# A tiled two-layer decoder in float32: the split of the Strassen weight differences is tied behind the next ordinary tile's split

## The chip, the cores and the metric

The kernel runs on one core of one Trainium2 chip. The metric is the device time of one execution in microseconds, as a median over runs. Five engines work side by side, each on its own list of instructions in the order of that list, with semaphores between them: TensorE (PE, matrix products; PEld is its loading of weights), VectorE (DVE), ScalarE (ACT), GpSimd (POOL) and SyncE (SP), which here issues the weight transfers.

## The reference

Two layers on 256 tokens of width 2048, all in float32. Layer 0 is a recurrent block (RG-LRU), layer 1 is sliding-window attention; behind each stands a gated feed-forward block. The change lies in the first matrix product of that block alone.

```python
def swiglu_ffn(x, g, w_in, w_out):
    h = rms_norm(x, g)
    gate, up = jnp.split(h @ w_in, 2, axis=-1)
    return x + (jax.nn.silu(gate) * up) @ w_out
```

## The kernel before

**Split products.** Each weight tile of 128x1024 float32 comes from memory into one of four buffers `raw0` to `raw3`. ACT casts it into `hi` (type fp32r), DVE subtracts `raw - hi` into `lo`, and each product is made of three matmuls: hi by hi, hi by lo, lo by hi. `hi` and `lo` have four buffers each, used in turn, so tile i+4 may only be cast when PE has done with tile i, and raw tile i+4 may only be loaded when ACT, DVE and POOL have read tile i.

**Strassen tiles.** In the product with `w_in` of each feed-forward block, the first four of 22 groups of output features (`NS = 4`) are computed with seven block products in place of eight. Each of these 32 *Strassen tiles* (four groups of eight) needs differences of its weight blocks: POOL makes two 128x512 tiles out of `raw` in three operations (`sums`, L279 to L281), ACT casts each (L288), DVE subtracts (L289). These land in one of two sets of buffers. A Strassen tile's own cast and split cover 768 columns only (`split`, L297 and L298); an ordinary tile's cover 1024 (L303 and L306). A Strassen tile has 21 matmuls (L472), an ordinary one 24 (L371). On PE one Strassen tile and one ordinary tile alternate (`OWN = 1`); I call two such neighbours a *pair*, and eight pairs a *group*. Within a Strassen tile in the middle of a group (L462 and L463) the first nine matmuls need `lo` and `hi` alone, the next six the first difference tile, the last six the second.

**Around a group's end.** When a Strassen group has ended, DVE combines four PSUM banks (`fast`: `s<-b,t` and `s<-b,s` at L132, then two L136). When a group of ordinary tiles has ended, DVE has a *burst* of six small operations, four `h<-b,rstd` that read PSUM and two `s<-h,h`. The Strassen tiles also need sums of the activations (`form`, L501 to L504 on POOL, a cast on ACT and a subtraction on DVE), which are made in advance, the last two while the first Strassen tiles run.

**What sets the order.** `stream` walks through all tiles: at step i it writes the load of tile i+4, then the split of tile i+3, then the split of the differences of tile i+2, then the products of tile i, with background tasks between. A scheduler then orders the instructions of each engine by its own estimate of when their inputs are there; the order written out is a priority, not the result. `issue_after(x)` ties the instructions written under it behind x, on the engine of x.

Of the kernel before, what the change touches and what calls it, by code (L numbers as in the profile page):

```python
# [12 lines left out]
F32 = mybir.dt.float32  # L13
F32R = mybir.dt.float32r
AF = mybir.ActivationFunctionType
ALU = mybir.AluOpType
# [33 lines left out]
class Trunk:  # L50
# [232 lines left out]
    def split_sums(self, i):  # L283

        if len(self.jobs[i]) > 2:
            s = self.jobs[i][2]["set"]
            for z, a, b in ((s[0], s[2], s[3]), (s[1], s[4], s[5])):
                self.nc.scalar.activation(a, z, AF.Copy)  # L288
                self.nc.vector.tensor_tensor(b, z, a.bitcast(F32), ALU.subtract)  # L289
            self.dve += 1400  # L290
            self.act += 1200

    def split(self, i):
        raw, hi, lo = self.raw[i % 4], self.hi[i % 4], self.lo[i % 4]
        if len(self.jobs[i]) > 2:
            q = slice(T, 1024)
            self.nc.scalar.activation(hi[:, q], raw[:, q], AF.Copy)  # L297
            self.nc.vector.tensor_tensor(lo[:, q], raw[:, q], hi[:, q].bitcast(F32), ALU.subtract)  # L298
            return
        n = 512 if i < 3 else 1024  # L300
        for c in range(0, 1024, n):
            q = slice(c, c + n)
            high = self.ins(self.nc.scalar.activation(hi[:, q], raw[:, q], AF.Copy))  # L303
            if i == 1:
                self.opening = high
            self.nc.vector.tensor_tensor(lo[:, q], raw[:, q], hi[:, q].bitcast(F32), ALU.subtract)  # L306

    def warm(self):

# [1059 lines left out]
```

## Time and profile before

| | us |
|---|---|
| median of three runs | 2023.03 (2022.57 to 2026.29) |
| the profiled execution | 2024.98 |
| its span, first to last instruction | 2023.2 |
| PE busy | 1983.6 (98%) |
| DVE busy | 1421.7 (70%) |
| ACT busy | 1126.1 (56%) |
| POOL busy | 384.5 (19%) |

The profile has the program's time line in 40 slices; POOL is busy in two stretches, the two stages with Strassen tiles (about 290 to 515 us and 1275 to 1490 us), and idle or nearly so in most of the rest. "Start us" counts from the span's first instruction; `s<-b,t` reads "written tile <- read tiles" with the buffers' numbers left out; x12 are twelve instructions of one kind that follow each other; `[1.84 <-ACT s L288]` says that the engine sat idle for 1.84 us before the row, until that ScalarE instruction was done. "DVE s L289 <- ACT s L288: 9.4, 6, 1.9" in the table of waits is 9.4 us in total, 6 times, 1.9 us the longest.

### The profile page before, as it was taken

The page shows a single profiled execution, that of the slowest core. Times are in us where ns is not written, and L with a number is a line of the kernel's source. Part 1 is how long each engine was busy: PE and PEld are TensorE (multiplying, and loading weights), DVE is VectorE, ACT ScalarE, POOL GpSimd, SP SyncE. Part 2 cuts the span into 40 slices and gives each one's busy share as a digit, 9 for nine tenths or more (in the row PEclk, how much of TensorE's full clock was granted, in tenths as well). Part 3 has the DMA queues.
Part 4 walks back from the last instruction along what each step waited for, and adds up shares of the span by engine and source line. Part 5 has one row for each costly group of instructions (what it writes and reads, how often), then busy time and mean ns, then how long its engine had stood idle before and what let it go on. Part 6 is the DMA issues. An engine that isn't in the chain of part 4 may idle for free.

```text
span 2023.2 us, 40996 instructions
## 1 busy us (share of the span) xinstructions
PE 1983.6 (98%) x16696; PEld 1940.0 (96%) x16696; DVE 1421.7 (70%) x2089; ACT 1126.1 (56%) x1762; POOL 384.5 (19%) x356
## 2 busy tenths in 40 slices
PE   9999998999999999999999999989999999999999
PEld 9999998989999999999999889989999999999999
DVE  8988979999565565545667767889976556554553
ACT  6799766555444444434556776655555445444342
POOL 0000137774000000000002453577700000000000
PEclk9999999999999999999999999999999999999999
DMA  7555655555655555555555435455565555566663
GB/s 275 190 182 184 212 171 169 184 175 185 197 196 192 194 195 191 193 195 196 194 185 175 136 126 167 157 181 177 173 201 193 194 196 189 197 197 201 207 208 126
DMA packets 106204, 377.15 MB, mean 186 GB/s; under 512 B 11936, under 2 KB 14368, under 8 KB 106016
## 3 DMA queue, kind: packets, MB, share of 16 engines
q1 hardware_dynamic: 105408, 373.88, 55.8%
q8 instruction: 130, 2.13, 0.4%
q10 hardware_dynamic: 608, 0.66, 0.1%
q14 instruction: 58, 0.48, 0.1%
HBM read 371.88 MB, written 2.10 MB: 185 GB/s over the span
## 4 chain that ended last, share of the span: by engine, by line
PE 79%; DVE 9%; POOL 4%; issue 3%; DMA 2%; ACT 2%; DVEq 0%; ACTq 0%; POOLq 0%; SPq 0%
PE b L371 73%; DVE s L289 2%; DMA raw<-in_ffn_in 2%; DVE lo L306 2%; PE b L472 2%; POOL s L279 2%; DVE lo L298 2%; PE b L382 1%; DVE s L132 1%; PE b L862 1%; PE b L379 1%; ACT hi L303 1%; ACT s L123 1%; PE b L1048 1%; POOL s L281 0%
## 5 line engine op out<-in xcount | busy, mean ns | idle before, releaser
L371 PE MATMUL b<-s,hi 128*128 128x256 f32 (+1 forms) x9470 | 1304.5, 284 | 2.4 <-ACT hi L303 1.1
L371 PEld LDWEIGHTS b<-s,hi 128*128 128x128 f32 x9470 | 1203.2, 188 | 25.5 <-ACT hi L303 1.8
L306 DVE TENSOR_TENSOR lo<-raw,hi 128x1024 fp32r<-128x1024 f32 (+1 forms) x643 | 799.3, 1246 | 493.5 <-ACT hi L303 490.9
L303 ACT ACTIVATE hi<-raw 128x1024 fp32r<-128x1024 f32 (+1 forms) x643 | 675.7, 1054 | 608.1 <-PE b L371 560.9
L371 PE MATMUL b<-s,lo 128*128 128x256 f32 x4992 | 753.6, 278 | 3.8 <-DVE lo L306 3.7
L371 PEld LDWEIGHTS b<-s,lo 128*128 128x128 f32 x4992 | 654.4, 189 | 5.3 <-DVE lo L306 4.8
L279 POOL TENSOR_TENSOR s<-raw 128x512 f32<-128x512 f32 x64 | 128.2, 2003 | 110.9 <-DMA raw<-in_ffn_in 101.5
L289 DVE TENSOR_TENSOR s<-s,s 128x512 fp32r<-128x512 f32 x128 | 132.4, 1058 | 20.2 <-ACT s L288 20.2
L1138 POOL TENSOR_TENSOR s<-s 128x128 f32<-128x128 f32 x32 | 14.8, 463 | 635.3 <-ACT s L123 632.6
L288 ACT ACTIVATE s<-s 128x512 fp32r<-128x512 f32 x128 | 78.8, 624 | 79.0 <-POOL s L281 40.6
L472 PE MATMUL b<-s,s 128*128 128x256 f32 x768 | 108.2, 285 | 7.7 <-DVE s L289 7.7
L472 PEld LDWEIGHTS b<-s,s 128*128 128x128 f32 x768 | 98.3, 190 | 10.0 <-DVE s L289 9.7
L472 PE MATMUL b<-hi,s 128*128 128x256 f32 x384 | 82.6, 285 | 5.5 <-DVE s L132 5.5
L123 ACT ACTIVATE s<-s 128x256 fp32r<-128x256 f32 (+3 forms) x164 | 64.3, 432 | 34.8 <-POOL s L504 22.5
L298 DVE TENSOR_TENSOR lo<-raw,hi 128x768 fp32r<-128x768 f32 x64 | 77.1, 1205 | 0.8 <-ACT hi L297 0.8
L281 POOL TENSOR_TENSOR s<-raw,s 128x256 f32<-128x256 f32 x64 | 73.2, 1143 | 5.0
L132 DVE TENSOR_TENSOR s<-s,s 128x256 fp32r<-128x256 f32 (+3 forms) x132 | 61.1, 491 | 17.1 <-ACT s L123 16.9
L502 POOL TENSOR_TENSOR s<-s 128x128 f32<-128x128 f32 x16 | 14.7, 916 | 302.1 <-ACT s L123 302.1
L472 PEld LDWEIGHTS b<-hi,s 128*128 128x128 f32 x384 | 65.4, 191 | 6.7 <-DVE s L132 6.7
L280 POOL TENSOR_TENSOR s<-raw,s 128x256 f32<-128x256 f32 x64 | 66.6, 1041 | 5.0
L123 ACT ACTIVATE s<-x,par 128x256 fp32r<-128x256 f32 (+1 forms) x112 | 52.7, 498 | 17.7 <-DVE x L132 11.2
L297 ACT ACTIVATE hi<-raw 128x768 fp32r<-128x768 f32 x64 | 53.3, 833 | 15.0 <-DMA raw<-in_ffn_in 6.3
(121 smaller groups left out, 1170.7 us busy)
## 6 DMA issues: line engine op xcount, KB each, us to landing
raw<-in_ffn_in SPq DMA_DIRECT2D x352, 512.0 KB, 3.4
raw<-in_ffn_out SPq DMA_DIRECT2D x176, 512.0 KB, 3.3
raw<-in_lru_in SPq DMA_DIRECT2D x62, 512.0 KB, 3.6
raw<-in_lru_out SPq DMA_DIRECT2D x32, 512.0 KB, 4.4
raw<-in_w_q SPq DMA_DIRECT2D x32, 512.0 KB, 3.3
raw<-in_w_o SPq DMA_DIRECT2D x32, 512.0 KB, 3.3
raw<-in_gate SPq DMA_DIRECT2D x8, 512.0 KB, 3.5
raw<-in_kv SPq DMA_DIRECT2D x8, 512.0 KB, 3.3
```

The costliest lines, as they stand in the source:

```text
L123: self.nc.scalar.activation(out, in_, func, **kw)
L132: self.nc.vector.tensor_tensor(out, a, b, op)
L279: tt(two(s[0][:, :]), b[:, 0:3:2, :], b[:, 1::-1, :], ALU.subtract)
L280: tt(s[1][:, 0:T], raw[:, 2 * T:3 * T], s[0][:, 0:T], ALU.subtract)
L281: tt(s[1][:, T:2 * T], raw[:, 3 * T:4 * T], s[1][:, 0:T], ALU.subtract)
L288: self.nc.scalar.activation(a, z, AF.Copy)
L289: self.nc.vector.tensor_tensor(b, z, a.bitcast(F32), ALU.subtract)
L298: self.nc.vector.tensor_tensor(lo[:, q], raw[:, q], hi[:, q].bitcast(F32), ALU.subtract)
L303: high = self.ins(self.nc.scalar.activation(hi[:, q], raw[:, q], AF.Copy))
L306: self.nc.vector.tensor_tensor(lo[:, q], raw[:, q], hi[:, q].bitcast(F32), ALU.subtract)
L371: self.nc.tensor.matmul(*args, **kw)
L472: self.nc.tensor.matmul(ps[b][:, h * T:h * T + T], w[i], m[j], start=b not in st["begun"], stop=c == ND // 2 - 1 and i == 1, skip_group_ch ...
```

## The change

`split` keeps the cast and the subtraction that it wrote last in `self.behind`, and `split_sums` ties the cast of each difference tile behind that cast, and its subtraction behind that subtraction. Since step i writes the split of tile i+3 just ahead of the differences of tile i+2, a Strassen tile's differences go behind the split of the ordinary tile that follows it.

```diff
@@ split_sums
             for z, a, b in ((s[0], s[2], s[3]), (s[1], s[4], s[5])):
-                self.nc.scalar.activation(a, z, AF.Copy)
-                self.nc.vector.tensor_tensor(b, z, a.bitcast(F32), ALU.subtract)
+                with self.tc.issue_after(self.behind[0]):
+                    self.nc.scalar.activation(a, z, AF.Copy)
+                with self.tc.issue_after(self.behind[1]):
+                    self.nc.vector.tensor_tensor(b, z, a.bitcast(F32), ALU.subtract)
@@ split
-            self.nc.scalar.activation(hi[:, q], raw[:, q], AF.Copy)
-            self.nc.vector.tensor_tensor(lo[:, q], raw[:, q], hi[:, q].bitcast(F32), ALU.subtract)
+            high = self.nc.scalar.activation(hi[:, q], raw[:, q], AF.Copy)
+            low = self.nc.vector.tensor_tensor(lo[:, q], raw[:, q], hi[:, q].bitcast(F32), ALU.subtract)
+            self.behind = [self.ins(high), self.ins(low)]
             return
...
-            self.nc.vector.tensor_tensor(lo[:, q], raw[:, q], hi[:, q].bitcast(F32), ALU.subtract)
+            low = self.nc.vector.tensor_tensor(lo[:, q], raw[:, q], hi[:, q].bitcast(F32), ALU.subtract)
+            self.behind = [high, self.ins(low)]
```

The instructions and their number stay the same on every engine. The order on PE and on SP is the same; DVE and ACT differ within the two Strassen stages, POOL at one place. Line numbers of the change are a little higher: its L291 is L289 of before, its L300 is L298, its L309 is L306, its L505 to L508 are L501 to L504.

DVE in the first stage, in the middle of a group, before (`lo2` and `lo0` belong to Strassen tiles, `lo3` and `lo1` to ordinary ones; `s5` and `s50` are the differences for `lo2`, `s28` and `s29` those for `lo0`):

```order
L298 TENSOR_TENSOR lo2_81<-raw2_73,hi2_77 128x768
L289 TENSOR_TENSOR s5_3724<-s2_3721,s4_3723 128x512
L289 TENSOR_TENSOR s50_3726<-s3_3722,s30_3725 128x512
L306 TENSOR_TENSOR lo3_82<-raw3_74,hi3_78 128x1024
L298 TENSOR_TENSOR lo0_79<-raw0_71,hi0_75 128x768
L289 TENSOR_TENSOR s28_3718<-s41_3715,s38_3717 128x512
L289 TENSOR_TENSOR s29_3720<-s19_3716,s39_3719 128x512
L306 TENSOR_TENSOR lo1_80<-raw1_72,hi1_76 128x1024
```

The same place in the change:

```order
L300 TENSOR_TENSOR lo2_81<-raw2_73,hi2_77 128x768
L309 TENSOR_TENSOR lo3_82<-raw3_74,hi3_78 128x1024
L291 TENSOR_TENSOR s5_3724<-s2_3721,s4_3723 128x512
L291 TENSOR_TENSOR s50_3726<-s3_3722,s30_3725 128x512
L300 TENSOR_TENSOR lo0_79<-raw0_71,hi0_75 128x768
L309 TENSOR_TENSOR lo1_80<-raw1_72,hi1_76 128x1024
L291 TENSOR_TENSOR s28_3718<-s41_3715,s38_3717 128x512
L291 TENSOR_TENSOR s29_3720<-s19_3716,s39_3719 128x512
```

The two difference tiles have moved from ahead of the ordinary tile's `lo` to behind it, in each pair; ACT's casts have moved in the same way.

DVE in the first stage, at the last burst (four rows that write `h4` to `h7`, two that write `s52`; `s12` is a split of an earlier result), before:

```order
L298 TENSOR_TENSOR lo2_81<-raw2_73,hi2_77 128x768
L289 TENSOR_TENSOR s5_3724<-s2_3721,s4_3723 128x512
L289 TENSOR_TENSOR s50_3726<-s3_3722,s30_3725 128x512
L132 TENSOR_TENSOR h4_99<-b2_85,rstd1_104 128x256
L132 TENSOR_TENSOR h5_100<-b2_85,rstd1_104 128x256
L132 TENSOR_TENSOR s12_5940<-s23_5455,s12_5940 128x256
L132 TENSOR_TENSOR s52_5605<-h4_99,h5_100 128x256
L132 TENSOR_TENSOR h6_101<-b1_84,rstd1_104 128x256
L132 TENSOR_TENSOR h7_102<-b1_84,rstd1_104 128x256
L306 TENSOR_TENSOR lo3_82<-raw3_74,hi3_78 128x1024
L132 TENSOR_TENSOR s52_5605<-h6_101,h7_102 128x256
L298 TENSOR_TENSOR lo0_79<-raw0_71,hi0_75 128x768
```

The same place in the change:

```order
L300 TENSOR_TENSOR lo2_81<-raw2_73,hi2_77 128x768
L132 TENSOR_TENSOR s12_5940<-s23_5455,s12_5940 128x256
L132 TENSOR_TENSOR h4_99<-b2_85,rstd1_104 128x256
L132 TENSOR_TENSOR h5_100<-b2_85,rstd1_104 128x256
L132 TENSOR_TENSOR s52_5605<-h4_99,h5_100 128x256
L132 TENSOR_TENSOR h6_101<-b1_84,rstd1_104 128x256
L132 TENSOR_TENSOR h7_102<-b1_84,rstd1_104 128x256
L309 TENSOR_TENSOR lo3_82<-raw3_74,hi3_78 128x1024
L132 TENSOR_TENSOR s52_5605<-h6_101,h7_102 128x256
L291 TENSOR_TENSOR s5_3724<-s2_3721,s4_3723 128x512
L291 TENSOR_TENSOR s50_3726<-s3_3722,s30_3725 128x512
L300 TENSOR_TENSOR lo0_79<-raw0_71,hi0_75 128x768
```

Here the two difference tiles of `lo2` have moved behind the whole burst and the ordinary tile's `lo3`, and stand just ahead of the next Strassen tile's `lo0`; the bursts of the other groups look alike in both kernels.

POOL at the start of the first stage (`s53` is the last sum of activations, `s41` and `s19` are the differences of the third Strassen tile), before:

```order
L504 TENSOR_TENSOR s23_3853<-s21_3852,s23_3853 128x128
L501 TENSOR_TENSOR s53_3861<-s52_3860 128x128
L503 TENSOR_TENSOR s53_3861<-s53_3861,s52_3860 128x128
L504 TENSOR_TENSOR s53_3861<-s52_3860,s53_3861 128x128
L279 TENSOR_TENSOR s41_3715<-raw0_71 128x512
L280 TENSOR_TENSOR s19_3716<-raw0_71,s41_3715 128x256
L281 TENSOR_TENSOR s19_3716<-raw0_71,s19_3716 128x256
```

The same place in the change:

```order
L508 TENSOR_TENSOR s23_3853<-s21_3852,s23_3853 128x128
L279 TENSOR_TENSOR s41_3715<-raw0_71 128x512
L280 TENSOR_TENSOR s19_3716<-raw0_71,s41_3715 128x256
L281 TENSOR_TENSOR s19_3716<-raw0_71,s19_3716 128x256
L505 TENSOR_TENSOR s53_3861<-s52_3860 128x128
L507 TENSOR_TENSOR s53_3861<-s53_3861,s52_3860 128x128
L508 TENSOR_TENSOR s53_3861<-s52_3860,s53_3861 128x128
```

The third Strassen tile's differences have moved ahead of the last sum of activations, which DVE and ACT wait for.

## The prediction, made before the change was run

> **What bounds the kernel now.** I read the time by stages first, then who waits for whom inside the two Strassen stages. In the table by stages the columns are the stretch, its length, then busy time and number of instructions of PE, PEld, DVE, ACT and POOL, then the granted clock, the DMA share and GB/s.
>
> ```profile
> 290.00:515.00 225.00, 208.39 (x1716) 203.15 (x1715) 205.57 (x231) 126.97 (x200) 141.68 (x104) 0.99 0.54 178
> 515.00:1150.00 635.00, 634.74 (x5379) 619.78 (x5378) 387.43 (x596) 325.00 (x495) 28.68 (x40) 1.00 0.57 188
> 1275.00:1490.00 215.00, 199.18 (x1632) 194.98 (x1631) 197.10 (x220) 122.50 (x191) 139.99 (x104) 0.98 0.54 176
> ```
>
> The stretch between the stages shows PE with no gap: 634.74 of 635. The two Strassen stages leave PE idle for 225 - 208.39 = 16.6 us and 215 - 199.18 = 15.8 us. Nothing that the change moves lies elsewhere, so these 32.4 us are the most it could win. DVE is busy for 91% of the first stage and 92% of the second; it is what PE waits for there. The change aims at what DVE itself waits for (first the row of stage 1, then that of stage 2):
>
> ```profile
> DVE s L289 <- ACT s L288: 9.4, 6, 1.9
> DVE s L289 <- ACT s L288: 10.7, 7, 1.9
> ```
>
> A difference tile stands early in DVE's list, its cast is late because POOL is late, and DVE idles for 20.1 us in all while the ordinary tile's split, which could run, stands behind it. What POOL does meanwhile decides what that idle time is worth. DVE first, then POOL, in one such place:
>
> ```profile
> 366.88 1.22 DVE L306 TENSOR_TENSOR lo<-raw,hi 128x1024 fp32r<-128x1024 f32 x1
> 368.35 0.95 DVE L298 TENSOR_TENSOR lo<-raw,hi 128x768 fp32r<-128x768 f32 x1
> 371.14 0.69 DVE L289 TENSOR_TENSOR s<-s,s 128x512 fp32r<-128x512 f32 x1 [1.84 <-ACT s L288]
> 373.13 1.11 DVE L289 TENSOR_TENSOR s<-s,s 128x512 fp32r<-128x512 f32 x1 [1.30 <-ACT s L288]
> 374.17 1.76 DVE L306 TENSOR_TENSOR lo<-raw,hi 128x1024 fp32r<-128x1024 f32 x1
> ...
> 365.23 5.22 POOL L279 TENSOR_TENSOR s<-raw 128x512 f32<-128x512 f32 x1 [2.87 <-DMA raw<-in_ffn_in]
> 370.52 0.74 POOL L280 TENSOR_TENSOR s<-raw,s 128x256 f32<-128x256 f32 x1
> 371.34 1.09 POOL L281 TENSOR_TENSOR s<-raw,s 128x256 f32<-128x256 f32 x1
> 372.39 1.30 POOL L279 TENSOR_TENSOR s<-raw 128x512 f32<-128x512 f32 x1
> ```
>
> POOL's L279 takes 5.22 us here and 1.30 us seven microseconds later. It stretched while DVE worked without a break, and it ended at 370.45, 1.15 us after DVE fell idle at 369.30 (368.35 + 0.95), not far from the 1.28 us that it takes at its shortest. DVE pays as well: the same subtraction takes 1.22 us with POOL stretched, and 1.76 us with POOL at work beside it. So the two take turns at something they share. Over a group that adds up. The shortest and median times of each form between 364 and 459 us:
>
> ```profile
> L306 DVE TENSOR_TENSOR lo<-raw,hi x17: 1211/1219/1759, 363.7 to 458.5; 128x1024 fp32r<-128x1024 f32 x17
> L298 DVE TENSOR_TENSOR lo<-raw,hi x16: 944/952/2050, 365.4 to 455.4; 128x768 fp32r<-128x768 f32 x16
> L289 DVE TENSOR_TENSOR s<-s,s x32: 674/1220/1787, 364.8 to 457.1; 128x512 fp32r<-128x512 f32 x32
> L279 POOL TENSOR_TENSOR s<-raw x16: 1284/1548/5687, 365.2 to 453.3; 128x512 f32<-128x512 f32 x16
> L280 POOL TENSOR_TENSOR s<-raw,s x16: 735/1068/1339, 370.5 to 454.7; 128x256 f32<-128x256 f32 x16
> ...
> 406.36 0.39 PE L472 MATMUL b<-hi,s 128*128 128x256 f32 x1 [1.06 <-DVE s L132]
> 453.63 0.39 PE L472 MATMUL b<-hi,s 128*128 128x256 f32 x1 [1.06 <-DVE s L132]
> ```
>
> One pair at the shortest times costs DVE 1.21 + 0.94 + 2 x 0.67 = 3.50 us and POOL 1.28 + 0.74 + 0.74 = 2.76 us (L281 taken as L280, the same shape); eight pairs cost 50.1 us one after the other. A group lasts 453.63 - 406.36 = 47.27 us. The pair DVE and POOL is as good as full, and the 3.14 us of DVE's idle time in this group were not free time: POOL worked in them.
>
> By the page "SBUF — State Buffer" of the Trainium skill, section "Who interferes with whom", a DVE instruction with two inputs in SBUF and a GpSimd instruction that reads SBUF hold one read port in turn, each for its whole length. The rows above agree. The rule speaks against this change: what DVE no longer idles it would wait for POOL later, so that by the rule none of the 20.1 us comes back, and by the rows of the first rival below a third of it.
>
> **The change part by part.** No instruction is added or removed, and the lists of PE and SP are the same, so the sum has three terms: where a difference tile gets later for PE, where DVE and POOL get further, and the start.
>
> A stage's end is set by its last wait of PE for DVE, because each wait puts PE back on DVE's time. So the first term is read at the last burst. DVE, then PE, of stage 1, then of stage 2:
>
> ```profile
> 479.77 2.38 DVE L289 TENSOR_TENSOR s<-s,s 128x512 fp32r<-128x512 f32 x2
> 487.63 1.49 DVE L298 TENSOR_TENSOR lo<-raw,hi 128x768 fp32r<-128x768 f32 x1
> 484.56 1.59 PE L472 MATMUL b<-s,s 128*128 128x256 f32 x12
> 489.18 0.39 PE L472 MATMUL b<-lo,s 128*128 128x256 f32 x1 [0.18 <-DVE lo L298]
> ...
> 1473.39 1.49 DVE L298 TENSOR_TENSOR lo<-raw,hi 128x768 fp32r<-128x768 f32 x1
> 1469.14 1.59 PE L472 MATMUL b<-s,s 128*128 128x256 f32 x12
> 1474.93 0.39 PE L472 MATMUL b<-lo,s 128*128 128x256 f32 x1 [0.96 <-DVE lo L298]
> ```
>
> Before, both difference tiles are ready at 479.77 + 2.38 = 482.15, and PE uses them from 484.56 on. In the change they stand just ahead of the next `lo0`, which before starts at 487.63; the same work lies ahead of that point in both kernels, so they end there. The twelve matmuls follow each other at about 0.117 us ((1.59 - 0.28) / 11, with 0.28 for one matmul), and the eighth is the first that needs the second tile's `lo` part: 484.56 + 7 x 0.117 = 485.38. PE then waits 487.63 - 485.38 = 2.25 us. The wait of 0.18 us behind it goes, since PE comes there later than `lo0`. Net **+2.1 us**. In stage 2 likewise 1473.39 - 1469.96 = 3.43 us, less 0.96: **+2.5 us**. What is queued behind the waiting differences on DVE is the next `lo0`, which PE needs last of all.
>
> Second term, how much further DVE and POOL get before that point. In the other bursts POOL waits for a transfer while DVE does work that does not slow POOL (POOL of stage 1, POOL of stage 2, DVE of stage 1):
>
> ```profile
> 388.25 2.10 POOL L279 TENSOR_TENSOR s<-raw 128x512 f32<-128x512 f32 x1 [2.66 <-DMA raw<-in_ffn_in]
> 1373.27 2.35 POOL L279 TENSOR_TENSOR s<-raw 128x512 f32<-128x512 f32 x1 [1.25 <-DMA raw<-in_ffn_in]
> 386.06 0.74 DVE L132 TENSOR_TENSOR h<-b,rstd 128x256 f32<-128x256 f32 x2
> 387.30 0.75 DVE L132 TENSOR_TENSOR h<-b,rstd 128x256 f32<-128x256 f32 x2
> ```
>
> In the change the burst comes ahead of two difference tiles, about 2.3 us earlier, when POOL is still at work; and the transfer for a Strassen tile starts 2 to 3 us after the one ahead of it in place of about 1 us (one `lo` apart before, a `lo` and two differences apart now), so that it lands sooner. POOL can then use up to 0.74 + 0.75 = 1.5 us per burst. I take 1.4 us for the burst shown, and 0.8 us for the three others with a wait like the 1.25 us: **-2.2 us** for stage 1, **-1.6 us** for stage 2. From below this is nothing (POOL waits there still), from above 1.5 us each. The idle time itself I take at nothing, from 0 to the third that the next part prices.
>
> Third, the start of stage 1. POOL now makes the third tile's differences ahead of the last activation sum (POOL, ACT, DVE, PE):
>
> ```profile
> 312.58 1.74 POOL L279 TENSOR_TENSOR s<-raw 128x512 f32<-128x512 f32 x1
> 312.64 0.63 ACT L123 ACTIVATE s<-s 128x512 fp32r<-128x512 f32 x1 [2.24 <-POOL s L504]
> 312.21 2.65 DVE L132 TENSOR_TENSOR s<-s,s 128x512 fp32r<-128x512 f32 x2
> 314.49 1.58 PE L472 MATMUL b<-s,s 128*128 128x256 f32 x12
> ```
>
> The three differences are 2.8 us at their shortest, so the sum's cast moves from 312.64 to 315.4 or later, DVE's second L132 behind it from 314.86 to about 317.7, and the `lo3` and the difference pair queued behind that on DVE end near 320, where PE wants them from 314.49 on. PE waits some 5 us there, but its later waits in this stage shrink by most of it, since they end on DVE's time; what is left is how far DVE falls behind. That is nothing if all that POOL does in the gap is spared DVE later, and half of the 3.7 us that the three operations take at their median times (1.55 and twice 1.07), 1.9 us, if it is not; I take **+1.0 us**. At the start of stage 2 one `lo` more stands ahead of the first pair of differences, for up to 1.2 us; as DVE does the same work there in another order, I take nothing.
>
> Sum: stage 1 +2.1 - 2.2 + 1.0 = +0.9, stage 2 +2.5 - 1.6 + 0 = +0.9, together +1.8 us. The profiled execution took 2024.98 us (span 2023.2), 1.95 us over the median of the runs, 2023.03; as the term is a difference, it goes onto the median: **2024.8 us**. A measurement of this kernel can tell about 0.2%, 4 us, from no change.
>
> **The rivals.** *Faster: the idle time does come back.* Beside one POOL operation of 0.74 us a DVE instruction grows by 0.43 (0.68 to 1.11) or 0.54 us (1.22 to 1.76), 58 to 73% of it; if DVE fills its gap, about a third is left as gain: 3.3 of 9.4 and 3.7 of 10.7 us. With the sum above: +1.8 - 7.0 = -5.2, so 2017.8 us. For it speaks that the growth is less than POOL's time; against it that 50.1 us of work stand in 47.3.
>
> *Slower: the differences are late at the bursts and nothing pays for it.* If POOL's transfer has still not landed when the earlier burst comes, the second term is gone: +2.1 + 2.5, with 1.9 and 1.2 us at the starts at their dear ends, +7.7, so 2030.7 us. It decides as soon as POOL falls idle during the burst as it does before. For it speaks how much POOL waits for transfers in stage 1, 49.1 us; against it the wider spacing of the transfers.
>
> ```profile
> POOL s L279 <- DMA raw<-in_ffn_in: 49.1, 19, 11.9
> ```
>
> *No effect:* the lists of DVE and ACT do differ, so only the chance is left that nothing changes by more than the scatter; that is in the forecast.
>
> **How the numbers follow.** My forecast 0.47, the faster rival 0.24, the slower one 0.29. The faster one lies beyond -4 us at its price, the slower one beyond +4 us; so faster by over 0.2% 0.25, within 0.46, slower 0.29. The range, 2017 to 2031, takes in both prices, and leaves out only a much larger gain or loss in every group.
>
> **What would show it.** Right: DVE's waits for L288 fall from 20.1 us to a few, L306 and L289 grow on the mean, groups still last about 47 us, and PE waits for L289 at each burst for 2 to 3 us. Wrong on the fast side: groups of 45 us or less. Wrong on the slow side: POOL still waiting for the transfer in the bursts, and groups of over 47.5 us. The whole argument would be wrong if DVE and POOL were seen at their shortest times side by side.

## The result, and the profile after

| | before | with the change |
|---|---|---|
| median of 18 runs each, us | 2023.13 | 2019.1 |
| ratio, 95% interval | | 0.9979, 0.9972 to 0.9986 |
| ratio in a later comparison (c_after) | | 0.9985, 0.9976 to 0.9994 |
| profiled execution, us (span) | 2024.98 (2023.2) | 2021.92 (2020.1) |
| stage 1, first to last Strassen matmul, us | 192.1 | 193.1 |
| stage 2, the same | 192.7 | 188.6 |

The change makes the kernel faster by 3 to 4 us where I had forecast +1.8 us (slower). In the profile all of the gain lies in stage 2, which I had forecast at +0.9 us as well. Busy times by stages of the changed kernel, in the columns of the prediction's first fence:

```profile
290.00:515.00 225.00, 208.30 (x1710) 203.28 (x1710) 208.18 (x230) 125.62 (x198) 145.64 (x104) 0.98 0.54 178
515.00:1150.00 635.00, 634.68 (x5379) 619.61 (x5378) 386.76 (x591) 325.51 (x495) 28.23 (x40) 1.00 0.57 188
1275.00:1490.00 215.00, 201.18 (x1668) 197.45 (x1667) 207.70 (x222) 123.49 (x193) 141.22 (x104) 0.98 0.56 183
```

The stretch between the stages is as before. In stage 2 PE does 36 matmuls more in the same 215 us (x1668 for x1632). The waits of stage 1, in the changed kernel (total, times, longest):

```profile
DVE s L291 <- ACT s L289: 4.4, 3, 1.9
...
POOL s L279 <- DVE s L291: 28.2, 15, 3.5
POOL s L279 <- DMA raw<-in_ffn_in: 24.5, 10, 11.9
```

DVE's wait for the differences' casts falls from 9.4 to 4.4 us, and in stage 2 this row is gone (10.7 us before). Half of POOL's wait for transfers, 49.1 us before, is now a wait for the difference buffers that DVE has still to read. PE at the last burst, of stage 1 and of stage 2:

```profile
477.04 1.58 PE L476 MATMUL b<-s,s 128*128 128x256 f32 x11 [1.70 <-DVE s L291]
483.04 0.38 PE L476 MATMUL b<-s,s 128*128 128x256 f32 x1 [0.64 <-ACT s L289]
484.46 2.47 PE L476 MATMUL b<-s,s 128*128 128x256 f32 x11 [1.04 <-DVE s L291]
...
1466.81 1.58 PE L476 MATMUL b<-s,s 128*128 128x256 f32 x11 [1.03 <-DVE s L291]
1472.89 1.57 PE L476 MATMUL b<-s,s 128*128 128x256 f32 x11 [0.59 <-DVE s L291]
```

PE waits there for difference tiles, as forecast, but for 0.64 + 1.04 = 1.7 us in stage 1 (the rows at 483.04 and 484.46) and 1.0 us in stage 2 (1466.81), where 2.25 and 3.43 us were worked out. The waits stand at the first two of the twelve matmuls, not at the eighth: it is the first difference tile that comes late. The rows at 477.04 and 1472.89 belong to the Strassen tiles ahead of and behind that one.

POOL at the two last bursts, before and then in the change:

```profile
484.45 1.30 POOL L279 TENSOR_TENSOR s<-raw 128x512 f32<-128x512 f32 x1 [0.71 <-DVE h L132]
1470.20 1.30 POOL L279 TENSOR_TENSOR s<-raw 128x512 f32<-128x512 f32 x1 [2.16 <-DVE s L132]
...
484.49 1.67 POOL L279 TENSOR_TENSOR s<-raw 128x512 f32<-128x512 f32 x1 [3.47 <-DVE s L291]
1466.84 1.68 POOL L279 TENSOR_TENSOR s<-raw 128x512 f32<-128x512 f32 x1 [3.46 <-DVE s L291]
```

The prediction had POOL at work through the earlier bursts. Here it stands idle longer than before, because the difference buffers that it needs next are read by DVE only behind the burst.

What I had not looked at stands at the start of stage 2. Before the change, ACT, then DVE, then POOL:

```profile
1280.96 0.63 ACT L288 ACTIVATE s<-s 128x512 fp32r<-128x512 f32 x1 [3.27 <-POOL s L279]
1281.50 0.37 ACT L123 ACTIVATE t<-b 128x256 f32<-128x256 f32 x1
1282.60 0.64 ACT L288 ACTIVATE s<-s 128x512 fp32r<-128x512 f32 x1 [0.73 <-POOL s L281]
...
1281.90 0.95 DVE L132 TENSOR_TENSOR x<-x,t 128x256 f32<-128x256 f32 x1 [2.95 <-ACT t L123]
1306.27 1.75 DVE L147 RECIPROCAL rstd<-nt 128x258 f32<-128x258 f32 x1
...
1289.53 0.99 POOL L502 TENSOR_TENSOR s<-s 128x128 f32<-128x128 f32 x1 [3.08 <-ACT s L123]
1304.46 1.34 POOL L281 TENSOR_TENSOR s<-raw,s 128x256 f32<-128x256 f32 x1
1308.78 1.47 POOL L279 TENSOR_TENSOR s<-raw 128x512 f32<-128x512 f32 x1 [2.99 <-DMA raw<-in_ffn_in]
```

The same places after:

```profile
1278.78 0.39 ACT L123 ACTIVATE t<-b 128x256 f32<-128x256 f32 x1
...
1279.88 0.42 DVE L132 TENSOR_TENSOR x<-x,t 128x256 f32<-128x256 f32 x1
1303.13 1.76 DVE L147 RECIPROCAL rstd<-nt 128x258 f32<-128x258 f32 x1
...
1288.35 0.61 POOL L506 TENSOR_TENSOR s<-s 128x128 f32<-128x128 f32 x1 [0.33 <-ACT s L123]
1303.88 0.74 POOL L281 TENSOR_TENSOR s<-raw,s 128x256 f32<-128x256 f32 x1
1306.97 1.40 POOL L279 TENSOR_TENSOR s<-raw 128x512 f32<-128x512 f32 x1 [2.35 <-DVE s L291]
```

Two things differ. Before, ACT stood 3.27 + 0.73 = 4.0 us at the first tile's casts, waiting for POOL, while the copy from PSUM that the residual needs (`t<-b`) and the activations for the last sums were queued behind; DVE waited 2.95 us for that `t`, and POOL 3.08 us for the activations. In the change the casts stand behind the ordinary tile's, and all three waits are gone or small. And the reciprocal, a DVE instruction with one input, ran before while POOL waited for a transfer (1305.80 to 1308.78); now POOL's L281 runs beside it at its shortest time, 0.74 us, and POOL's work covers most of it.

### The profile page after: what moved, and what is told of

The parts are those of the page before. It is cut to its first block, busy times and chain, and to the rows that moved or that the text cites. A ratio compares the mean times of both kernels' runs of the same rounds, so it can differ in the third digit from the quotient of the medians.

```text
span 2020.1 us, 40931 instructions
## 1 busy us (share of the span) xinstructions
PE 1982.2 (98%) x16696; PEld 1939.0 (96%) x16696; DVE 1433.0 (71%) x2089; ACT 1124.9 (56%) x1762; POOL 389.4 (19%) x356
## 4 chain that ended last, share of the span: by engine, by line
PE 85%; DVE 9%; issue 2%; ACT 2%; POOL 1%; DMA 0%; DVEq 0%; ACTq 0%; POOLq 0%
PE b L375 77%; PE b L476 4%; DVE lo L309 3%; DVE s L291 2%; DVE lo L300 1%; PE b L386 1%; DVE s L132 1%; PE b L866 1%; ACT s L123 1%; ACT hi L306 1%; DVE s L136 1%; PE b L383 1%; PE b L1052 1%; DVE h L132 0%; DVE s L1120 0%
## 5 line engine op out<-in xcount | busy, mean ns | idle before, releaser
L309 DVE TENSOR_TENSOR lo<-raw,hi 128x1024 fp32r<-128x1024 f32 (+1 forms) x643 | 807.7, 1258 | 500.0 <-ACT hi L306 498.0
L306 ACT ACTIVATE hi<-raw 128x1024 fp32r<-128x1024 f32 (+1 forms) x643 | 676.3, 1054 | 654.8 <-PE b L375 608.4
L279 POOL TENSOR_TENSOR s<-raw 128x512 f32<-128x512 f32 x64 | 121.0, 1890 | 105.8 <-DVE s L291 54.9
L476 PE MATMUL b<-s,s 128*128 128x256 f32 x768 | 114.0, 290 | 22.1 <-DVE s L291 19.3
L476 PEld LDWEIGHTS b<-s,s 128*128 128x128 f32 x768 | 100.6, 192 | 28.1 <-DVE s L291 23.9
L291 DVE TENSOR_TENSOR s<-s,s 128x512 fp32r<-128x512 f32 x128 | 112.1, 912 | 4.4 <-ACT s L289 4.4
L300 DVE TENSOR_TENSOR lo<-raw,hi 128x768 fp32r<-128x768 f32 x64 | 95.4, 1491 | 0.0
L280 POOL TENSOR_TENSOR s<-raw,s 128x256 f32<-128x256 f32 x64 | 81.7, 1277 | 6.3 <-DVE s L291 1.4
L132 DVE TENSOR_TENSOR s<-s,s 128x256 fp32r<-128x256 f32 (+3 forms) x132 | 68.1, 545 | 19.7 <-ACT s L123 19.5
L289 ACT ACTIVATE s<-s 128x512 fp32r<-128x512 f32 x128 | 73.6, 617 | 11.6 <-POOL s L281 7.1
L281 POOL TENSOR_TENSOR s<-raw,s 128x256 f32<-128x256 f32 x64 | 72.1, 1126 | 5.0
```

The source lines that it names most:

```text
L132: self.nc.vector.tensor_tensor(out, a, b, op)
L279: tt(two(s[0][:, :]), b[:, 0:3:2, :], b[:, 1::-1, :], ALU.subtract)
L280: tt(s[1][:, 0:T], raw[:, 2 * T:3 * T], s[0][:, 0:T], ALU.subtract)
L281: tt(s[1][:, T:2 * T], raw[:, 3 * T:4 * T], s[1][:, 0:T], ALU.subtract)
L300: low = self.nc.vector.tensor_tensor(lo[:, q], raw[:, q], hi[:, q].bitcast(F32), ALU.subtract)
L309: low = self.nc.vector.tensor_tensor(lo[:, q], raw[:, q], hi[:, q].bitcast(F32), ALU.subtract)
```

## The experiments

`n` counts the Strassen tiles, 0 to 31 in stage 1 and 32 to 63 in stage 2. Most experiments tie only some of them, by one condition in two places (code left out is marked `...`):

```diff
-            s = self.jobs[i][2]["set"]
+            s, n = self.jobs[i][2]["set"], sum(len(j) > 2 for j in self.jobs[:i])
...
-                with self.tc.issue_after(self.behind[0]):
+                with self.tc.issue_after(self.behind[0]) if n < 32 else nullcontext():
                     self.nc.scalar.activation(a, z, AF.Copy)
-                with self.tc.issue_after(self.behind[1]):
+                with self.tc.issue_after(self.behind[1]) if n < 32 else nullcontext():
```

For the others only the condition is given. Stage lengths are from the first to the last Strassen matmul in the profile, the fifth split is the start of the fifth `lo` of a Strassen tile of stage 2, in us behind the stage's first Strassen matmul. The microseconds are the ratio times 2023; each has an interval of about 1.8 us to either side.

| kernel | tied | stage 1 | stage 2 | fifth split | ratio to before | us |
|---|---|---|---|---|---|---|
| before | none | 192.1 | 192.7 | 25.6 | 1 | |
| e_s1 | n < 32 | 191.4 | 192.1 | 25.2 | 0.9997 | -0.6 |
| e_s2 | n >= 32 | 190.4 | 188.0 | 23.2 | 0.9982 | -3.6 |
| e_last | n % 32 != 29 | 192.1 | 188.6 | 22.8 | 0.9977 | -4.7 |
| e_first | n != 0 | 191.3 | 188.8 | 23.0 | 0.9977 | -4.7 |
| e_burst | n % 8 != 5 | 191.5 | 188.9 | 22.8 | 0.9986 | -2.8 |
| e_mid | n % 32 not in (5, 13, 21) | 193.0 | 190.6 | 23.1 | 0.9994 | -1.2 |
| e_st2 | not 32 <= n < 36 | 193.2 | 192.1 | 25.4 | 0.9998 | -0.4 |
| e_only4 | 32 <= n < 36 | 193.6 | 188.1 | 22.8 | 0.9982 | -3.6 |
| e_t32 | n == 32 | 193.1 | 189.9 | 23.9 | 0.9990 | -2.0 |
| e_t33 | 33 <= n < 36 | 193.3 | 191.6 | 24.5 | 0.9993 | -1.4 |
| c_after | all | 193.3 | 189.5 | 23.0 | 0.9985 | -3.0 |
| f_pool | all, POOL's order as before | 190.8 | 188.6 | 23.2 | 0.9975 | -5.1 |
| f_only5 | n == 0 or 32 <= n < 36, POOL's order as before | 190.8 | 190.7 | 23.2 | 0.9978 | -4.5 |

Profiles of the same lists of instructions differ too. Five kernels have the order of before in stage 1 (before, e_s2, e_only4, e_t32, e_t33), and that stage lasts 190.4 to 193.6 us in them; so one profile's stage 1 says little, and the ratios decide.

**One stage alone.** e_s1, condition `n < 32`, and e_s2, `n >= 32`:

> The tie in the first Strassen stage only; the second as before. Stages by first and last Strassen matmul: before 191.6 and 192.2 us, with the change 192.6 and 188.1 us. Theory A, each stage keeps what its own trace shows and they do not touch each other: +1.0 us on the kernel before, so about 2024.1, the gain is gone. Theory C, part of each stage's difference is where the lowered clock fell (each such stretch loses 1.7 us, one in stage 1 before and two after): about -0.7 on the kernel before, so 2022.4. The prediction's sum for this stage is +0.9, the same as A.

> The tie in the second Strassen stage only. Theory A: -4.1 us on the kernel before, about 2019.0. Theory C (one stretch of lowered clock fewer in this stage by chance, 1.7 us): -2.4, about 2020.7. The prediction's sum for this stage: +0.9, about 2024.

Stage 1 gives 0.9997 (0.9989 to 1.0006), stage 2 gives 0.9982 (0.9973 to 0.9990). The gain is that of stage 2. Whether the theory with the lowered clock or the one without is nearer can't be told from these intervals; stage 2 with the tie has 188.0 to 189.5 us in every profile in which its ties are left whole and POOL's work is the same.

**The last burst (first term).** e_last, `n % 32 != 29`:

> As the changed kernel, but the differences of the Strassen tile at the last burst of each stage are not tied, so that they stand ahead of the burst again. First term of the prediction as it was sized (2.1 + 2.5 us): -4.6 on the changed kernel, about 2014.5. First term as the trace of the changed kernel shows PE's waits there (3.4 less 0.2 us in stage 1, 1.6 less 1.0 in stage 2): up to -3.8, nearly all in stage 1. Rival: what the waits cost is paid back by POOL working beside the burst, so that taking the tie away there changes nothing (within 1 us).

0.9977 (0.9968 to 0.9986) stands for no difference to the changed kernel. PE at the last burst of stage 1 in e_last:

```profile
484.85 1.21 PE L375 MATMUL b<-s,lo 128*128 128x256 f32 x8 [1.31 <-DVE lo L309]
488.13 1.58 PE L476 MATMUL b<-s,s 128*128 128x256 f32 x11 [0.92 <-DVE s L291]
```

With the difference tiles ahead of the burst again, PE waits for the ordinary `lo` and for the next differences instead: the wait changes its name. The rival had the time right, that the tie there neither costs nor wins; its reason, POOL at work beside the burst, is not what the changed kernel shows, where POOL stood idle for 3.47 us there.

**The start of stage 1 (third term).** e_first, `n != 0`, brings back POOL's order of before:

> As the changed kernel, but the differences of the very first Strassen tile of stage 1 are not tied; POOL then makes the last activation sum ahead of the third tile's differences, as before the change. Third term of the prediction as sized: -1.0 on the changed kernel, about 2018.1, with the waits of 2.07 and 0.95 us at 316 to 317 us gone. Larger if these two waits were a loss in full: -3.0, about 2016.1. Rival: DVE only gets as far by the group's end as before, so the waits come back later in the group and the time stays (within 0.5 us).

0.9977, as the changed kernel: the rival's number. Its reason is doubtful, since with the first tile tied and POOL's order as before (f_pool below) the start is faster than in either kernel.

**All bursts.** e_burst, `n % 8 != 5`:

> As the changed kernel, but in each group the differences of the Strassen tile at the burst are not tied (eight tiles of 64), so that they stand ahead of the burst again. If the gain is made at the bursts, by their PSUM-reading work now lying beside POOL's (0.8 us a burst by the traces so far), it is lost again at the six bursts that are not a stage's last, +4.8 us on the changed kernel, about 2024, nothing left of the change; at the last bursts loss and gain cancel, as with only those two untied. If DVE's idle time comes back in every pair, wherever it stands, only a quarter of the tiles lose it: within 1 us of the changed kernel, about 2019.5. The prediction's own terms, -2.2 and -1.6 for bursts against +2.1 and +2.5 for late tiles, would give -0.8 on the changed kernel.

0.9986 (0.9977 to 0.9995) beside 0.9985 of c_after on the same chip: no loss. The change's gain is not made at the bursts.

**The start of stage 2.** e_st2 takes the tie away from its first four tiles, e_only4 ties these four and no other:

> As the changed kernel, but the first four Strassen tiles of stage 2 are not tied. Theory: the start of stage 2 is the step that the prediction missed (taken at 0, up to +1.2; by DVE's progress up to the fifth Strassen tile's split it is -2.5), because the reciprocal and its neighbours, with one input, found POOL waiting for a transfer before and find it at work in the change. Then +2.5 on the changed kernel, about 2021.6, and the fifth split 25.4 us behind the stage's first matmul instead of 22.9. Rival: the gain is spread over all pairs of stage 2: +0.5, within the scatter.

> As the kernel before, but with the tie for the first four Strassen tiles of stage 2 only. If the start of stage 2 is a gain by itself: -2.5 us on the kernel before, ratio about 0.9988, the fifth split at 22.9 us behind the stage's first matmul. If it needs the rest of the tie (the lead is lost again at the next waits of DVE for ACT): DVE is ahead at the fifth split, but the stage is as long as before (192.1 to 192.7) and the ratio is 1.

Without these four tiles the other sixty give 0.9998 (0.9989 to 1.0007); the four alone give 0.9982 (0.9973 to 0.9991). Four tiles of 64 make the whole gain. In e_st2, ACT, DVE, POOL:

```profile
1281.53 0.63 ACT L289 ACTIVATE s<-s 128x512 fp32r<-128x512 f32 x1 [3.40 <-POOL s L279]
...
1306.51 1.75 DVE L147 RECIPROCAL rstd<-nt 128x258 f32<-128x258 f32 x1
...
1304.10 1.07 POOL L281 TENSOR_TENSOR s<-raw,s 128x256 f32<-128x256 f32 x1
1309.55 1.30 POOL L279 TENSOR_TENSOR s<-raw 128x512 f32<-128x512 f32 x1 [4.38 <-DMA raw<-in_ffn_in]
```

Both features of before are back: ACT's wait of 3.40 us, and a reciprocal with POOL idle from 1305.17 to 1309.55.

e_st2 also answers the prediction's main question, what DVE's idle time is worth. Its stage 2 has no wait of DVE for the differences' casts any more (10.7 us before), and yet it lasts 192.1 us, as DVE's busy time from 1275 to 1490 us grew from 197.10 to 205.83 us. e_only4 still has half of that wait, and its stage lasts 188.1 us:

```profile
DVE s L291 <- ACT s L289: 5.7, 4, 1.9
```

**The two apart.** e_t32 ties the first of the four, e_t33 the other three:

> As the kernel before, but with the tie for one tile only, the first Strassen tile of stage 2. Of the four tiles that by themselves gave the whole gain, it is the one whose casts stood on ScalarE ahead of the last activations and waited there for GpSimd (3.27 and 0.73 us). Theory A1, that wait is the cause: GpSimd's activation sums start about 1.2 us earlier against the stage's first matmul, DVE's wait of 1.0 us for the cast of the last one goes, the split of the stage's first tile (L300) starts 2.0 to 2.5 us ahead of the first matmul instead of 0.8 to 1.1, and about half of the gain is there: -1.2 to -2 us, ratio 0.9990 to 0.9994. Theory A2, the reciprocal beside an idle GpSimd is the cause: nothing, ratio 1, and the fifth split stays at 25.2 to 25.6 us. If the two are not a sum (the earlier start alone lets the reciprocal fall beside GpSimd's work, or is lost without it): -3.7 or 0.

> As the kernel before, but with the tie for the second, third and fourth Strassen tile of stage 2 only. These put the reciprocal (1.75 us on DVE, one input) ahead of two difference tiles. Theory A2: it then runs while GpSimd still works, the 1.6 us in which neither DVE's two-input work nor GpSimd ran at 1306 to 1308 us go, and the stretch from the first to the fifth split shrinks from 26.4 to about 25.1 us: -1.2 to -2 us, ratio 0.9990 to 0.9994. Theory A1 (ScalarE's wait for the first tile's differences is the cause): nothing, ratio 1.

0.9990 (0.9981 to 0.9999) and 0.9993 (0.9984 to 1.0002), -2.0 and -1.4 us, together -3.4, beside the -3.6 of the four. The fifth split says the same: it comes 1.7 and 1.1 us earlier than before, and 2.8 us earlier in e_only4. In e_t32 POOL's wait ahead of the activation sums is down to 0.3 us (first fence), but the reciprocal still falls into POOL's wait for a transfer (second fence, DVE, then POOL):

```profile
POOL s L506 <- ACT s L123: 0.3, 1, 0.3
```

```profile
1303.01 1.75 DVE L147 RECIPROCAL rstd<-nt 128x258 f32<-128x258 f32 x1
...
1301.19 1.34 POOL L281 TENSOR_TENSOR s<-raw,s 128x256 f32<-128x256 f32 x1
1305.61 1.38 POOL L279 TENSOR_TENSOR s<-raw 128x512 f32<-128x512 f32 x1 [3.08 <-DMA raw<-in_ffn_in]
```

In e_t33 it is the other way round, ACT, DVE, POOL:

```profile
1281.30 0.63 ACT L289 ACTIVATE s<-s 128x512 fp32r<-128x512 f32 x1 [3.52 <-POOL s L279]
...
1304.02 1.75 DVE L147 RECIPROCAL rstd<-nt 128x258 f32<-128x258 f32 x1
...
1304.78 0.74 POOL L281 TENSOR_TENSOR s<-raw,s 128x256 f32<-128x256 f32 x1
```

So each of the two effects is there without the other, and each carries about half. The second interval just includes 1; that the two add up rests on three ratios and three profiles. That the reciprocal alone makes the second half is argued from these rows: the tie moves three tiles' differences, and no run moves the reciprocal by itself.

**How far DVE and POOL take turns.** In e_twice POOL's third operation is written twice, with the same result:

```diff
-        tt(s[1][:, T:2 * T], raw[:, 3 * T:4 * T], s[1][:, 0:T], ALU.subtract)
+        tt(s[1][:, T:2 * T], raw[:, 3 * T:4 * T], s[1][:, 0:T], ALU.subtract); tt(s[1][:, T:2 * T], raw[:, 3 * T:4 * T], s[1][:, 0:T], ALU.subtract)
```

> As the changed kernel, but POOL's third operation of each Strassen tile (L281, 0.74 us at its shortest) is issued twice, 64 more operations and nothing else. If DVE and POOL take turns and are as good as full, each costs its whole 0.74 us, 5.9 us a group, less the 0.3 us a group that is idle now: about +45 us, 2064. If a DVE instruction grows only by 58 to 73% of what POOL does beside it: +27 to +34 us, about 2050. If they only look coupled and PE and the buffers set the pace: POOL has 25% of the stages to itself, so within 5 us of the changed kernel.

2051.51 us, 30.9 over c_after's 2020.61 on the same chip: 0.48 us for each of the 64 operations of 0.74 us, 65%, within the 58 to 73% of the second expectation. The stages grew by 15.1 and 16.0 us. So they do take turns, but about a third of such an operation costs no time.

**The changed kernel again.** c_after is the changed kernel without an edit.

> The changed kernel once more, for a second profile of it. In stage 1 the kernel of this program with the tie in stage 1 only had one stretch of lowered clock and 191.4 us, the first profile two and 193.1 us: 191.4 to 193.1 here, by the number of such stretches (1.7 us each). Stage 2 within 188.0 to 188.8 us as in the other four profiles with this order, if the gain there is not chance. Time 2019 to 2020.

2020.61 us, 0.9985: stage 2 was 189.5 us, 0.7 us over the most that was expected, stage 1 193.3, 0.2 us over, with three stretches of lowered clock.

**Groups that don't add up.** e_mid, `n % 32 not in (5, 13, 21)`:

> As the changed kernel, but the differences of the tile at a burst are not tied at the three bursts of a stage that are not its last (six tiles of 64). With all eight untied, DVE came to the split of the 25th Strassen tile 1.3 us earlier in stage 1 and 2.0 us earlier in stage 2 than in the changed kernel, and lost that in the last group. If groups add up: stage 1 about 191.0, stage 2 about 187 us, 2 to 3 us under the changed kernel, ratio to before about 0.997. Rival: DVE's progress in the earlier groups is no gain at the stage's end, since the last burst makes PE wait for POOL and the transfers in any case: within 1 us of the changed kernel, ratio 0.998 to 0.9985.

0.9994 (0.9985 to 1.0003): neither. Up to the last group the lists are those of e_burst. In stage 1 DVE's lead was there (139.5 us to the 25th split, 139.2 in e_burst, 140.6 in the changed kernel) and was lost in the last group; in stage 2 it was not (138.8, 135.6 and 138.1). Why the same lists ran differently there is open.

**POOL's order in stage 1.** In f_pool the lists of all engines are those of the changed kernel, but POOL makes the last activation sum ahead of the third tile's differences again; f_only5 has the same edit, with only the first tile of stage 1 and the first four of stage 2 tied:

```diff
-        tt(two(s[0][:, :]), b[:, 0:3:2, :], b[:, 1::-1, :], ALU.subtract)
+        with self.tc.issue_after(self.summed) if sum(len(j) > 2 for j in self.jobs[:i]) == 2 else nullcontext(): tt(two(s[0][:, :]), b[:, 0:3:2, :], b[:, 1::-1, :], ALU.subtract)
...
-        tt(s[3], a12, s[1], ALU.subtract)
+        self.summed = self.ins(tt(s[3], a12, s[1], ALU.subtract))
```

> The changed kernel, every engine's list the same but for one place: on GpSimd the third Strassen tile's differences of stage 1 are tied behind the last activation sum, as the order was before the change. In stage 1 before, ScalarE waits 4.2 and 0.74 us with the first tile's casts and DVE 3.9 us behind it, as in stage 2; the tie takes this away in both stages, but in stage 1 the changed kernel has a new wait of DVE of 3.6 us for the last sum's cast. Theory: the new wait is the third term (forecast +1.0) and it hides a gain like that of the first tile in stage 2 (-2.0): without it -2 us on the changed kernel, ratio to before about 0.9972, stage 1 about 1 to 2 us shorter. Rival: DVE makes up for the start by the group's end in any case, as leaving the first tile untied showed no difference: within 0.5 us of the changed kernel, ratio 0.998 to 0.9985.

> As the kernel before, but with the tie for the first tile of stage 1 and the first four tiles of stage 2 only, and the same order of GpSimd as before. If the starts are what the change gains by and the other 59 tiles add nothing: -3.6 (four tiles of stage 2) and -2 (first tile of stage 1), about -5.6 us on the kernel before, ratio 0.9972. If the start of stage 1 gives nothing: ratio 0.9982, as with the four tiles alone.

0.9975 (0.9966 to 0.9984) and 0.9978 (0.9969 to 0.9987): both lie between what their theories and their rivals gave, and the intervals reach both. DVE's wait for the last sum's cast, in the changed kernel and in f_pool:

```profile
314.50 0.69 DVE L132 TENSOR_TENSOR s<-s,s 128x512 fp32r<-128x512 f32 x1 [3.61 <-ACT s L123]
```

```profile
308.73 1.11 DVE L132 TENSOR_TENSOR s<-s,s 128x512 fp32r<-128x512 f32 x1 [1.02 <-ACT s L123]
```

The fifth split of stage 1 comes 24.0 us behind the stage's first Strassen matmul in f_pool, 25.4 to 26.3 in the four profiles with the changed kernel's lists there (26.2 and 26.3 in its own two), and 24.5 to 25.4 in the five with the order of before. So the swap on POOL costs 1.4 to 2.3 us there. In f_only5, where the first tile is the only one tied in that stage, the fifth split comes at 22.2 us: that tie alone saves 2.3 to 3.2 us, and the ties of the tiles behind it take 1.8 us back (24.0 less 22.2). f_pool has the lowest ratio measured; that it beats the changed kernel is likely by the trace, and not certain by the times, whose intervals overlap.

## Why the prediction was wrong

**What bounds the kernel: right in kind.** DVE and POOL hold each other up, and groups only went from 47.0 to 47.5 us to 45.7 to 46.7 (between the transposes at 364.15, 410.19 and 456.74, and 1347.07, 1393.80 and 1439.52). That none of DVE's idle time would come back was wrong for these groups: the 50.1 us of work in 47.3 already said that some of it overlaps. By the end of the kernel it held: sixty tied tiles, with no wait of DVE for the casts left in stage 2, were worth -0.4 us (e_st2). The run with the doubled operation puts the cost at 0.48 of 0.74 us. The rule of the Trainium skill ("SBUF — State Buffer", "Who interferes with whom"), each for its whole length, would give 0.74; the measurement decides.

**First term, late tiles at the last burst: right in kind, +2.1 and +2.5 a little small.** From the 31st split of a Strassen tile to the last Strassen matmul it is 9.4 to 9.5 us in stage 1 in the five profiles with the order of before, and 12.4 to 13.2 in those with the last burst's tile tied. In stage 2 it is 9.4 to 9.5 us in five of the six profiles in which that tile is not tied (11.8 in e_s1), and 12.4 in all in which it is. That is some +3 us in each stage. But putting these tiles back won nothing (e_last), since PE waits for the next work of DVE instead.

**Second term, DVE and POOL further ahead by then: larger, and not by the bursts.** From the fifth to the 31st split it is 155.9 to 159.2 us in stage 1 in the five profiles with the order of before, and 153.6 to 153.9 in the five with DVE's list of the change; in stage 2 157.8 and 155.0, then 152.5 to 154.1. On the means that is -4.3 and -3.1, where I had -2.2 and -1.6. Untying the bursts ahead of the last did not lose it: from the fifth to the 25th split e_burst takes 113.9 and 112.8 us, the kernels with these bursts tied 114.3 to 114.8 and 113.8 to 115.5. So my mechanism was wrong. The third of the idle time that the first rival priced would give (20.1 - 4.4) x 0.35 = 5.5 us of these 7.4; that this is where they come from is argued, not shown.

**Third term, the start of stage 1: mis-sized, with a gain I had not seen.** POOL's late sum costs 1.4 to 2.3 us at the fifth split, not 1.0, and the ties of the first tiles, above all of the first, whose casts no longer stand in ACT's way, give back about half of that (the fifth split comes at 25.1 us on the mean before, 26.0 in the change, 24.0 in f_pool). In all stage 1 came out at -0.6 us by the times, with an interval that holds the +0.9.

**The step that failed: "At the start of stage 2 one `lo` more stands ahead of the first pair of differences, for up to 1.2 us; as DVE does the same work there in another order, I take nothing."** It was worth -3.6 us by itself, nearly all of the gain, and the runs show what it consists of: the first tile's casts no longer make ACT wait for POOL ahead of work that DVE and POOL need (-2.0), and most of the reciprocal's 1.75 us now lies beside POOL's work (-1.4, with an interval that just includes nothing). The step looked at DVE's list alone. It also bounded the cost from one side: nothing to +1.2, without a reason that excluded a gain. Without these four tiles the change is within a measurement of nothing (-0.4 us, with an interval up to +1.4), a little under the +1.8 of my sum; with them it is faster.

**The rivals.** The faster one foresaw the time (2017.8 us for 2019.1 and 2020.6), but by another road: its gain in the middle of the stages came and was paid out again at the last burst, so that its number came near by luck. The slower one's condition, POOL idle in the bursts because its transfer has not landed, did not occur; but POOL did stand idle, most clearly in three of the eight bursts, for 3.1 to 3.5 us each, for difference buffers that DVE had still to read. No part of the prediction had that wait.

## What to carry to other kernels

When an instruction is moved back, look at what was queued *behind it on its own engine before*, and who waited for that; a cast that waits on a slow producer at the head of an in-order queue can hold up three engines at the point where one stage passes into the next. Starts of stages have work of another kind (here a norm, activation sums) and deserve their own timeline, not a line in the sum. And a change that touches 64 places may owe its result to four: untying the places by groups finds out faster than weighing the terms.

## What the runs showed of the hardware

The granted clock of PE fell for stretches of some microseconds within the Strassen stages. One in the profile of before, one of the changed kernel, each in a row of 4 us (columns as above):

```profile
1396.00:1400.00 4.00, 3.66 (x17) 3.47 (x18) 4.00 (x7) 3.69 (x7) 1.44 (x1) 0.57 0.67 216
```

```profile
1348.00:1352.00 4.00, 4.00 (x24) 4.00 (x23) 3.56 (x6) 2.82 (x5) 3.78 (x2) 0.57 0.63 210
```

Each loses 4 x 0.43 = 1.7 us of clock. In both kernels the profile has four in the two stages; where they fall differs from run to run of the same list of instructions. The page "TensorE: Matmul & The Clock Gate" of the Trainium skill ("What's actually happening") has half the rate until a busy window of about 3.4 us has gone by. Half of that, 1.7 us, is an estimate from the page's figures, and these two rows agree with it. The stretches do not decide the time: with the same lists in stage 1, the order of before, that stage lasted 193.1 to 193.6 us in the three profiles without any such stretch, and 190.4 and 192.1 us in the two with one. Whole kernels show it too: e_t33 had one such stretch in a span of 2022.1 us, c_after six in 2020.7 us. That PE waits for DVE here in any case, so that a stretch is taken out of a later wait, would explain it; it was not tried.
